# Hybrid attention block: q and k of a pair of heads as seven block products, computed ahead of attention

## The chip, the cores and the metric

One Trainium2 chip, one core of it. The metric is the device time of one execution of the program, in microseconds (us); the median of the runs is compared. Engines are named as in the profile: PE is the matrix engine, PEld its weight load, DVE the vector engine, ACT the scalar engine, POOL the GpSimd engine, SP the engine whose queue issues most DMAs.

## The reference

One decoder layer on x of 1024 tokens by 1024 channels, float32. What matters here:

```
h = rms_norm(x, attn_norm_w)
q, k, v, u, g = split(h @ w_in)            # 1024, 1024, 1024, 2048, 2048 columns
q, k = rms_norm over each 64 columns       # 8 heads, each with two 64-wide halves
p = softmax(q1 k1 / 8 + bias) - lam * softmax(q2 k2 / 8 + bias)     # causal
a = rms_norm(p @ v) * 0.2 ;   y_a = a @ w_proj_attn
c = silu(layer_norm(causal_depthwise_conv(u_a * sigmoid(u_b), 31 taps))) ;  y_b = c @ w_proj_conv
x = x + (sigmoid(g_a) * y_a + sigmoid(g_b) * y_b) @ w_out
x = x + (silu(gate) * up) @ w_down         # of rms_norm(x); 2816 wide
```

## The kernel before

**Numbers.** Each float32 operand of a product is kept as a high and a low part in the matrix engine's reduced type: `split_hi` is a copy on ACT (L120), `low` a subtraction on DVE (L125) or, while `low_by_pool` is set, on POOL (L131). A product is then three matmuls, high by high, high by low and low by high (`mm3`, L168 to L170). `hT_hi` and `hT_lo` hold the normalized input, transposed, in on-chip memory.

**Order of the work.** `first_stage` is a generator; the loop around it gives the depthwise convolution `due += 3.25` steps at every yield. It computes v in four items of 256 columns (`v_item`; V0 in `opening`), then u: the first 128 columns plainly, and the rest in seven `u_pair`s. A `u_pair` already uses a block scheme: the input's channels and tokens are split in two halves each, and seven block products of sums (`TS`, made once by `sums_of_h`) and of weight sums take the place of eight. Then come `Q0` (q and k of head 0) and `V3`. After that attention runs 64 steps, one for each head and each block of 128 queries, in the order of `ORDER`.

**q and k.** `q_item(h)` makes the 256 columns of one head by `gemm_N`: 8 token tiles, 8 channel tiles, 3 matmuls each, 128x256. ACT copies the result out of PSUM (L797) and makes 32 sums of squares (L800), DVE scales by the reciprocal root (L807), and `turn_qk` transposes on PE (L815, tile pQ), scales and splits, and moves half partitions by DMA on SP's queue. `late` holds these turns until their tiles are free.

**An attention step.** `scores(h, i)`: two halves, for each of them matmuls into one of three PSUM tiles `sc` (L1289, L1290), bias and running minimum on DVE (L1291), exponential on ACT (L1296); then both halves are combined on DVE (L1306). `turn` transposes the block of the step before (pT, L1328) and splits it; `weigh` multiplies by v after every second block (pW); `back` and `subln` normalize. Between them `more` puts one or two items of `fill`, which is the list `later`: Q1 to Q7 and the sixteen gates G0 to G15 (`g_item`, 128x512 matmuls, two halves of 24), so that PE has work while a step's softmax runs. The scheduler may move instructions against the program's order, by its own timeline, except where `after` holds them.

**Convolution.** Eight channel blocks, each one load, one first tap on ACT (L588) and 30 taps on DVE (L594, 240 in all); `add_tile` adds a finished block by a DMA on POOL's queue. The accumulator of the first `CONV_PSUM = 4` blocks lies in PSUM, in banks that attention's `sc` tiles take over when `bg.until((NKT - CONV_PSUM) * (CW + 1) - 1)` has drained them. The rest of the taps are spread over the attention steps by each step's estimated slack.

**Weights.** `ws` is the queue of weight tiles, loaded on SP's queue and split ahead of use; `wtiles` rotates three pairs `whi`, `wlo`.

Of the kernel before, what the change touches and what calls it, by code (L numbers as in the profile page):

```python
# [10 lines left out]
F32 = mybir.dt.float32  # L11
# [5 lines left out]
P = 128  # L17
# [40 lines left out]
def kernel(  # L58
# [48 lines left out]
    sm.tile([P, 32], F32, name="pad_sm", bufs=1)  # L107
# [148 lines left out]
    def vectors():  # L256
# [5 lines left out]
        dve.tensor_scalar(pcol("kn"), pcol("kn"), -(HD ** -0.5), None, op0=ALU.mult)  # L262
# [21 lines left out]

    def wtiles():
        return [wp.tile([P, 1024], F32R, tag=t_, name=nm(t_)) for t_ in ("whi", "wlo")]
# [89 lines left out]
    def gemm_N(o, halves, shi, slo, i):  # L376
# [8 lines left out]
    v_lo = [dr.tile([S, 256], F32, name=f"v_lo{j}") for j in range(4)]  # L385
    a_d = [dr.tile([P, S], F32, name=f"a_d{h}") for h in range(H)]
# [16 lines left out]
    last = ["Q0", "V3"]  # L403
    later = [
        ["Q1", "G0", "G1"],
        ["Q2", "G2", "G3"],
        ["Q3", "G4"],
        ["Q4", "G5", "G6"],
        ["Q5", "G7"],
        ["Q6", "G8", "G9"],  # L410
        ["Q7", "G10"],
        ["G11", "G12", "G13", "G14"],
        ["G15"],
    ]

    def loads_of(it):
        c = int(it[1:])
        if it[0] == "V":
            return ld_wide(win, [(V0 + 256 * c, 256)])
        if it[0] == "Q":  # L420
            return ld_wide(win, [(Q0 + c * P, P), (K0 + c * P, P)])
# [4 lines left out]
    for it in ["U0"] + first + last + [x_ for l_ in later for x_ in l_]:  # L426
        ws.plan(loads_of(it))
# [138 lines left out]
    CONV_PSUM = 4  # L566
# [67 lines left out]
    def g_item(c):  # L634
        w = ws.next()
        for sb in range(2):
            o = gemm_T(w, hT_hi, hT_lo, sb)
            sg = wp.tile([P, 512], F32, tag="sg", name=nm("sgg"), bufs=2)
            act.activation(sg[:], o[:], AF.Identity, bias=pcol("gate_b", c))
            nc.sync.dma_start(g_d[c][:, sb * 512 : (sb + 1) * 512], sg[:])  # L640
            yield


    def rsq(v, n, fast):

        r = sm.tile([P, 16], F32, tag="r", name=nm("r"))[:, :n]
        t = sm.tile([P, 16], F32, tag="t", name=nm("t"))[:, :n]
# [32 lines left out]
    def rstd_of(ss, n, scale, fast=False):  # L680
        v = sm.tile([P, 16], F32, tag="v", name=nm("v"))[:, :n]
# [104 lines left out]
    def q_item(h):  # L786
        halves = [ws.next(), ws.next()]
        t = {}
        T[h] = t
        for b in (1, 0):  # L790
            raw = qkp.tile([P, 4, 256], F32, tag="qkraw", name=nm("qkraw"), bufs=2)
            ss = sm.tile([P, 16], F32, tag="ss16", name=nm("ss16"))
            for i2 in range(2):
                o = pg()
                for e in range(2):
                    gemm_N(o[:, 256 * e : 256 * (e + 1)], halves, hT_hi, hT_lo, 4 * b + 2 * i2 + e)
                act.copy(raw[:, 2 * i2 : 2 * i2 + 2, :], o[:].rearrange("p (e c) -> p e c", c=256))  # L797
                jk = sm.tile([P, VD], F32, tag="jk", name=nm("jk"), bufs=1)[:, :HD]
                for g in range(8):
                    act.activation(  # L800
                        jk, o[:, g * HD : (g + 1) * HD], AF.Square, accum_out=ss[:, 8 * i2 + g : 8 * i2 + g + 1]
                    )
                if i2 == 0:
                    yield
            r = rstd_of(ss[:], 16, 1.0 / HD, fast=h > 0)
            r4 = raw[:].rearrange("p i (g d) -> p (i g) d", d=HD)
            dve.tensor_tensor(r4, r4, r.unsqueeze(2).to_broadcast([P, 16, HD]), op=ALU.mult)  # L807

            def turn_qk(z, key, b, raw):


                dma = nc.sync.dma_start
                pt = pm("pQ")
                for i in range(4):
                    pe.transpose(pt[:, i * P : (i + 1) * P], raw[:, i, z * P : (z + 1) * P], ident[:])  # L815
                w = pcol(key + "n")

                def part(j):
                    return qkp.tile([P, 512], F32R, tag=f"{key}s{j}", name=f"{key}s{j}_{h}_{b}", bufs=2 if key == "q" else 3)

                s1, s2 = part(1), part(2)
                act.activation(s1[:], pt[:], AF.Identity, scale=w)
                lo = part(3) if key == "q" else qkp.tile([P, 512], F32R, tag="klo", name=f"klo_{h}_{b}", bufs=1)
                dve.scalar_tensor_tensor(lo[:], pt[:], w, f32(s1[:]), op0=ALU.mult, op1=ALU.subtract)
                if key == "q":
                    dma(f32(s2[HD:, :]), f32(s1[HD:, :]))
                    lo2 = part(4)
                    for one, two in ((s1, s2), (lo, lo2)):
                        if one is lo:
                            dma(f32(two[HD:, :]), f32(one[HD:, :]))  # L830
                        dma(f32(two[:HD, :]), f32(one[HD:, :]))
                        dma(f32(one[HD:, :]), f32(one[:HD, :]))
                    t["q", b] = (s1, lo), (s2, lo2)
                else:
                    act.activation(s2[HD:, :], pt[HD:, :], AF.Identity, scale=w[HD:, :])
                    dma(f32(s2[:HD, :]), f32(lo[HD:, :]))
                    dma(f32(s1[HD:, :]), f32(lo[:HD, :]))
                    t["k", b] = s1, s2

            for z, key in ((1, "k"), (0, "q")):
                free = NT * (h - 1) + (0 if key == "k" and b else NT if key == "q" and not b else NT // 2)
                late.append((free if h else 0, lambda a_=(z, key, b, raw): turn_qk(*a_)))
            yield

    inatt = [False]
    MAKE = {"V": v_item, "U": u_item, "Q": q_item, "G": g_item}
# [179 lines left out]

    def first_stage():
# [6 lines left out]

        def weights_ahead():
            yield
            ws.ahead = 1
            ws.fetch()  # L1040
            yield
# [17 lines left out]
        for c in range(1, NKT):  # L1059
            ahead = ups[c] if c < NKT - 1 else weights_ahead()  # L1060
            next(ahead)
            A = yield from u_pair(c, A, ahead)
        st_ctx.close()
        tt_ctx.close()
# [8 lines left out]
        v_tiles[0] = v3_tiles  # L1073
        load_bias(0)
        ws.ahead = 2
        yield from run(last[:1])
        bg.until((NKT - CONV_PSUM) * (CW + 1) - 1)
        yield from run(last[1:])
# [155 lines left out]
    for _ in first_stage():  # L1234
# [7 lines left out]
        due += 3.25  # L1242
# [5 lines left out]
    low_by_pool[0] = False  # L1248
# [10 lines left out]
    V, AN, SSA, PT, ES, RL = {}, {}, {}, {}, {}, {}  # L1259

# [10 lines left out]
    def scores(h, i):  # L1271
# [7 lines left out]
        for j in range(2):  # L1279
            qh, ql = t["q", i // 4][j]  # L1280
            e = aps.tile([P, S], F32, tag="E", name=nm("E"), bufs=4)
# [16 lines left out]
            )  # L1298
        if h not in RL:
# [59 lines left out]
    def subln(h):  # L1359
        an = AN[h]  # L1360
        r = rstd_of(SSA[h][:], NT, 1.0 / VD, fast=True)
        dve.tensor_tensor(an[:], an[:], r.unsqueeze(2).to_broadcast([P, NT, VD]), op=ALU.mult)
# [26 lines left out]
    fill = run(it for l_ in later for it in l_)  # L1389
    plan = [sum(4 if it[0] == "Q" else 2 for it in l_) for l_ in later]  # L1390
# [744 lines left out]
```

## Time and profile before

| | |
|---|---|
| median of 3 runs | 1727.1 us (1726.74 to 1728.84) |
| profiled execution, span from first to last instruction | 1725.7 us; the page gives it no other time |
| PE busy | 1714.6 us, 99% of the span |
| DVE busy | 1275.4 us, 74% |
| ACT busy | 862.5 us, 50% |
| POOL busy | 219.1 us, 13% |

How to read it: the busy share is an average over stages. "Windows" are stretches of the span, with busy time of each engine in each. A group row gives line, engine, operation, output and inputs, count, then busy time and mean ns of one, then the idle time before it and what ended that. A matmul's record is longer than the time after which the next one starts, so for PE the spacing of starts in the timeline is the price of one.

### The profile page before, as it was taken

Reading aid. Unit: us, or ns where it says so; the run is one execution under the profiler, and the core shown is the slowest. Engines: PE = TensorE matmul, PEld = TensorE weight load, DVE = VectorE, ACT = ScalarE, POOL = GpSimd, SP = SyncE. Lnnn points to the kernel's source line nnn. Section 1 sums busy time; section 2 is a strip of 40 time slices with the busy share of each in tenths; the row PEclk is TensorE's granted clock in tenths of the full one; section 3 lists DMA queues with packets and bytes.
Section 4 is the critical chain, followed back from the end, with each engine's and each line's share of the span. In section 5 each row is a group of like instructions: output and inputs, shape, how many; then the busy total and the mean of one; then the engine's idle time right before and its main releaser. Section 6 shows DMA issues by size and latency. Waiting matters only on the chain.

```text
span 1725.7 us, 25863 instructions
## 1 busy us (share of the span) xinstructions
PE 1714.6 (99%) x9243; PEld 1477.9 (86%) x9243; DVE 1275.4 (74%) x2128; ACT 862.5 (50%) x1958; POOL 219.1 (13%) x207
## 2 busy tenths in 40 slices
PE   9999999999999999999999999999999999999999
PEld 7997889998998998988788888888888888888887
DVE  7675889898988888878687769966676666575544
ACT  5333335767777776756556325633333333333332
POOL 3997851000000000000000000000000000000000
PEclk9999999999999999999999999999999999999999
DMA  6344445336345344343973683245455445598663
GB/s 208 116 126 132 131 151 154 104 109 171 104 127 147 115 125 138 101 136 130 333 238 118 200 296 119 74 135 164 147 170 170 154 141 164 175 355 285 217 215 130
DMA packets 261604, 281.64 MB, mean 163 GB/s; under 512 B 16546, under 2 KB 181986, under 8 KB 261475
## 3 DMA queue, kind: packets, MB, share of 16 engines
q1 hardware_dynamic: 254160, 267.71, 48.3%
q0 software_dynamic: 5680, 9.39, 2.6%
q10 hardware_dynamic: 1634, 2.89, 0.5%
q8 instruction: 73, 1.20, 0.3%
q14 instruction: 57, 0.46, 0.1%
HBM read 181.84 MB, written 85.50 MB: 155 GB/s over the span
## 4 chain that ended last, share of the span: by engine, by line
PE 92%; DMA 3%; DVE 2%; ACT 1%; issue 1%; POOL 0%; SPq 0%; DVEq 0%; POOLq 0%; ACTq 0%
PE acc L980 29%; PE acc L488 12%; PE pg L168 12%; PE pg L169 12%; PE pg L170 12%; PE wo L1850 3%; PE sc L1290 2%; PE sc L1289 2%; PE pT L1328 2%; PE pg L1106 1%; DVE acc L594 1%; PE pW L168 1%; PE pW L169 1%; PE pW L170 1%; PE pQ L815 1%
## 5 line engine op out<-in xcount | busy, mean ns | idle before, releaser
L594 DVE SCALAR_TENSOR_TENSOR acc<-u,cw,acc 128x1023 f32<-128x1023 f32 (+14 forms) x240 | 303.4, 1264 | 23.2 <-ACT acc L588 20.7
L170 PE MATMUL pg<-whi,hT_lo 128*128 128x256 f32 x704 | 200.2, 285 | 0.0
L168 PE MATMUL pg<-whi,hT_hi 128*128 128x256 f32 x704 | 199.7, 285 | 0.4 <-DVE v L125 0.4
L169 PE MATMUL pg<-wlo,hT_hi 128*128 128x256 f32 x704 | 199.5, 284 | 0.0
L125 DVE TENSOR_TENSOR wlo<-draw,whi 128x1024 fp32r<-128x1024 f32 x75 | 91.7, 1223 | 83.4 <-ACT whi L120 78.9
L120 ACT CAST whi<-draw 128x1024 fp32r<-128x1024 f32 x75 | 79.1, 1055 | 129.5 <-PE acc L488 114.3
L169 PEld LDWEIGHTS pg<-wlo,hT_hi 128*128 128x128 f32 x704 | 134.4, 191 | 1.8
L170 PEld LDWEIGHTS pg<-whi,hT_lo 128*128 128x128 f32 x704 | 134.3, 191 | 1.8
L168 PEld LDWEIGHTS pg<-whi,hT_hi 128*128 128x128 f32 x704 | 134.0, 191 | 2.1 <-DVE v L125 0.6
L120 ACT CAST whi<-wraw 128x1024 fp32r<-128x1024 f32 x90 | 94.7, 1052 | 70.6 <-PE pg L169 32.6
L488 PE MATMUL acc<-wlo,whi 128*128 128x512 f32 x308 | 119.8, 389 | 0.0
L488 PE MATMUL acc<-whi,wlo 128*128 128x512 f32 x308 | 119.8, 389 | 0.0
L1296 ACT ACTIVATE E<-E,mn 128x640 f32<-128x640 f32 (+7 forms) x128 | 99.8, 781 | 30.8 <-DVE mn L1291 29.2
L168 PE MATMUL pg<-hT_hi,whi 128*128 128x512 f32 x288 | 114.4, 397 | 0.1
L169 PE MATMUL pg<-hT_lo,whi 128*128 128x512 f32 x288 | 113.7, 395 | 0.0
L170 PE MATMUL pg<-hT_hi,wlo 128*128 128x512 f32 x288 | 113.7, 395 | 0.0
L120 ACT CAST whi<-s 128x1024 fp32r<-128x1024 f32 x54 | 56.9, 1053 | 104.9 <-PE acc L980 101.8
L125 DVE TENSOR_TENSOR wlo<-wraw,whi 128x1024 fp32r<-128x1024 f32 x75 | 93.3, 1246 | 12.6 <-ACT whi L120 12.3
L1291 DVE CUSTOM_DVE_ANT_0 E<-sc,tb 128x512 f32<-128x512 f32 (+3 forms) x128 | 74.2, 585 | 33.2 <-PE pT L1328 16.1
L980 PE MATMUL acc<-h_hi,whi 128*128 128x512 f32 x240 | 93.4, 389 | 0.0
L980 PE MATMUL acc<-h_lo,whi 128*128 128x512 f32 x240 | 93.4, 389 | 0.0
L980 PE MATMUL acc<-h_hi,wlo 128*128 128x512 f32 x240 | 90.1, 389 | 0.0
(370 smaller groups left out, 4589.7 us busy)
## 6 DMA issues: line engine op xcount, KB each, us to landing
wraw<-in_w_gate_up_dram SPq DMA_DIRECT2D x44, 512.0 KB, 4.7
wraw<-in_w_in_dram SPq DMA_DIRECT2D x38, 512.0 KB, 4.0
qs<-qs SPq DMA_DIRECT2D x96, 128.0 KB, 2.3
wd<-in_w_down_dram SPq DMA_DIRECT2D x44, 256.0 KB, 3.1
tdT<-wd SPq DMA_DIRECT2D x88, 128.0 KB, 4.8
draw<-sdS SPq DMA_DIRECT2D x44, 256.0 KB, 3.7
draw<-tdT SPq DMA_DIRECT2D x44, 256.0 KB, 3.7
wraw<-in_w_in_dram SPq DMA_DIRECT2D x32, 256.0 KB, 3.3
```

What stands on the lines that cost most here:

```text
L120: act.copy(dst, src)
L125: last_lo[0] = dve.tensor_tensor(dst, src, f32(hi), op=ALU.subtract).ins
L168: pe.matmul(o, lh, rh, start=start, stop=False)
L169: pe.matmul(o, lh, rl, start=False, stop=False)
L170: last_mm[0] = pe.matmul(o, ll, rh, start=False, stop=stop).ins
L488: m = pe.matmul(o[s_][i][:], l_[:, ts], r_[:, 512:], start=start and j + y_ == 0, stop=j == n - 1 and y_ == 2, skip_group_check=not start,)
L594: dve.scalar_tensor_tensor(a_, us[c][:, : S - n], cw[:, c, t : t + 1], a_, op0=ALU.mult, op1=ALU.add)
L980: last_mm[0] = pe.matmul(o[:], a_[x_][:, k, :], b_[y_][:, k, :], start=start and k + x_ + y_ == 0, stop=k == 3 and x_ == 1, skip_group_che ...
L1289: pe.matmul(o[:, :w], qh[:, qs], k, start=True, stop=False)
L1291: dve.tensor_tensor_reduce(e[:, ks], o[:, :w], tb[:, S - nk + c0 : S - nk + c0 + w], 1.0, mn[:, j : j + 1] if c0 else 3.0e38, ALU.add, ALU ...
L1296: act.activation(e[:, :nk], e[:, :nk], AF.Exp, bias=mn[:, j : j + 1], scale=-1.0, accum_out=l[:, j : j + 1])
L1850: last_mm[0] = pe.matmul(o[s_][i][:], A[u_], B[v_], start=start and j + y_ == 0, stop=j == 3 and y_ == 2, skip_group_check=not start,).ins
```

## The change

Seven things, which go together.

1. `Q` items leave the list of fill work. A new stage `q_stage` between the last `u_pair` and `V3` computes q and k of two heads at a time (`q_pair`), by seven block products (`QSEVEN`) with the sums `TS` that the `u_pair`s use. A product is 4 token tiles by 4 channel tiles by 3 matmuls of 128x256. Sums of weights and the low parts are made on POOL (on DVE at the start of the first pair). Its `yield`s come after each product, so the convolution gets its 3.25 steps 28 times more.
2. The results go to memory (`qk_d`, 512 KB for a head and half of the tokens), with sums of squares by one Square on ACT and one reduction on DVE for each half. The reciprocal roots are made on DVE for six heads at once and for two (`qk_roots`).
3. Attention loads them back (`qk_load`, at steps 0 and 3 of the head before), scales them on POOL one step later (`qk_norm`), and turns them with the same `turn_qk`.
4. `later` is the sixteen gates alone. `g_item` yields after a quarter of a half (6 matmuls), and `more` runs once in the middle of `scores` and once behind it.
5. `turn` comes two steps behind `scores`, not one. Two weight tiles (`whi2`, `wlo2`) serve as fifth and sixth `E` tile, and the weights of attention rotate over two pairs.
6. `low_by_pool` stays set through attention, and `subln` multiplies on POOL, but for the last head.
7. `CONV_PSUM` is 6.

```diff
-        dve.tensor_scalar(pcol("kn"), pcol("kn"), -(HD ** -0.5), None, op0=ALU.mult)
+        dve.tensor_scalar(pcol("qn"), pcol("qn"), -0.125, None, op0=ALU.mult)
+        dve.tensor_scalar(pcol("kn"), pcol("kn"), 0.125 * HD ** -0.5, None, op0=ALU.mult)
...
     def wtiles():
-        return [wp.tile([P, 1024], F32R, tag=t_, name=nm(t_)) for t_ in ("whi", "wlo")]
+        z = next(wplace[0])
+        return [wp.tile([P, 1024], F32R, tag=f"{t_}{z}", name=nm(t_), bufs=1) for t_ in ("whi", "wlo")]
...
-    last = ["Q0", "V3"]
-    later = [["Q1", "G0", "G1"], ...
+    last = ["V3"]
+    later = [f"G{c}" for c in range(2 * NKT)]
...
-    CONV_PSUM = 4
+    CONV_PSUM = 6
...
     def g_item(c):
...
+                mm3(o[:], w[0][:, k, :], w[1][:, k, :], hT_hi[:, k, cs], hT_lo[:, k, cs], k == 0, k == NKT - 1)
+                if k % 2 and k < NKT - 1:
+                    yield
...
+    def qk_load(h, b):
+        raw = qkp.tile([P, 4, 256], F32, tag="qkraw", name=f"qkraw{h}_{b}", bufs=2)
+        nc.sync.dma_start(raw[:].rearrange("p i c -> p (i c)"), qk_d[h][b][:])
...
+    def qk_norm(h, b, raw):
+        r = rs[:, 32 * h + 16 * b : 32 * h + 16 * b + 16]
+        r4 = raw[:].rearrange("p i (g d) -> p (i g) d", d=HD)
+        (pool if h else dve).tensor_tensor(r4, r4, r.unsqueeze(2).to_broadcast([P, 16, HD]), op=ALU.mult)
...
+    QSEVEN = (
+        ("11", (0, 0), "b"),
+        ("12", (1, 0), "a"),
+        ("S2", 2, "b"),
+        ("S1", 1, "c"),
+        ("S3", 3, "b"),
+        ("S4", (1, 1), "c"),
+        ("22", 4, "b"),
+    )
...
+        def keep(k):
+            h, b = 2 * c + k[0], k[1]
+            t_ = out[k]
+            nc.sync.dma_start(qk_d[h][b][:], t_[:].rearrange("p i c -> p (i c)"))
+            for e in range(2):
+                jk = wp.tile([P, 512], F32, tag="sg", name=nm("qsq"), bufs=2)
+                act.activation(jk[:], t_[:, 2 * e : 2 * e + 2, :].rearrange("p i c -> p (i c)"), AF.Square)
...
+        for z, (a_, b_, s_) in enumerate(QSEVEN):
...
+            for i in range(4):
+                ts = slice(i * P, (i + 1) * P)
+                e, w = i // 2, slice(256 * (i % 2), 256 * (i % 2 + 1))
+                for k in range(4):
+                    for x_, y_ in ((0, 0), (0, 1), (1, 0)):
+                        last_mm[0] = pe.matmul(
+                            o[s_][e][:, w], Bz[x_][:, k, ts], hi_lo[y_][:, k, :],
...
+            if z == 0:
+                take((0, 0), "b")
+                if c == 0:
+                    less(raw["S1"], raw["21"], raw["22"], ALU.add, dve)
+                    less(raw["21"], raw["11"], raw["21"], eng=dve)
+                less(raw["11"], raw["S1"], raw["11"], eng=pool if c else dve)
+                low_by_pool[0] = c > 0
+                A["S2"] = q_split(raw["11"])
+                low_by_pool[0] = True
+            elif z == 1:
+                plus((0, 0), "a")
+                keep((0, 0))
+                A["S1"] = q_split(raw["S1"])
+            elif z == 2:
+                take((0, 1), "b")
+                A["S3"] = q_split(raw["21"])
+                less(raw["12"], raw["12"], raw["11"])
...
         st_ctx.close()
+        yield from q_stage()
...
     while late:
         late.pop(0)[1]()
-    low_by_pool[0] = False
     pcv_ctx.close()
...
+            if j == 0:
+                scm.append(last_mm[0])
+                amid()
...
-        dve.tensor_tensor(an[:], an[:], r.unsqueeze(2).to_broadcast([P, NT, VD]), op=ALU.mult)
+        eng = pool if h < H - 1 else dve
+        eng.tensor_tensor(an[:], an[:], r.unsqueeze(2).to_broadcast([P, NT, VD]), op=ALU.mult)
...
-        scores(h, i)
+        if h + 1 < H and n % NT in (0, 3):
+            raws[n % NT == 0] = qk_load(h + 1, int(n % NT == 0))
+        if h + 1 < H and n % NT in (1, 4):
+            qk_norm(h + 1, int(n % NT == 1), raws[n % NT == 1])
+        scores(h, i, lambda: more(p))
         scm.append(last_mm[0])
-        more((p + 1) // 2)
-        if n:
-            hp, ip = steps[n - 1]
+        more(p)
+        if n > 1:
+            hp, ip = steps[n - 2]
             turn(hp, ip)
```

More of the change, by code (lines that the diff above doesn't have):

```diff
@@ L784 @@
     late = []
[L786 to L845, printed above, removed]
@@ L1388 @@
     scm, weighs, backs, sublns = [], [], [], []
[L1389 to L1390 removed]
+    fill = run(later)
     def more(k):
[L1394 removed]
+        with after(scm[-7] if len(scm) >= 7 else None):
             for _ in range(k):
@@ L1468 @@
     n = len(steps)
+    wplace[0] = cycle((0, 1, 2))
+    turn(*steps[-2])
     group()
```

237 lines of the change are left out of this document (196 added, 41 removed).

## The prediction, made before the changed kernel was run

> **What bounds the kernel now.** I read the page's first parts, then windows, then single instructions in order of time.
>
> ```profile
> span 1725.7 us, 25863 instructions
> PE 1714.6 (99%) x9243; PEld 1477.9 (86%) x9243; DVE 1275.4 (74%) x2128; ACT 862.5 (50%) x1958; POOL 219.1 (13%) x207
> PE 92%; DMA 3%; DVE 2%; ACT 1%; issue 1%; POOL 0%; SPq 0%; DVEq 0%; POOLq 0%; ACTq 0%
> ```
>
> PE is busy 99% of the span and carries 92% of the chain that ended last. A busy PE may still be a waiting one, so the windows around the change, and PE's own waits in attention, come next (columns: stretch, then PE, PEld, DVE, ACT, POOL busy, the granted clock, DMA share and rate).
>
> ```profile
> 147.00:247.00 100.00, 100.00 (x447) 82.56 (x447) 84.54 (x79) 37.17 (x50) 72.48 (x45) 1.00 0.39 118
> 297.00:822.00 525.00, 522.13 (x3487) 477.30 (x3486) 447.48 (x985) 370.37 (x1215) 21.06 (x74) 1.00 0.45 128
> ...
> PE sc L1289 <- DMA ks<-klo: 1.1, 1, 1.1
> PE sc L1290 <- DMA qs<-qs: 0.8, 1, 0.8
> ```
>
> The stretches are the last five pairs of u, and attention; Q0 and V3 lie between. The granted clock is 1.00 in both. In attention PE's two long waits for others make 1.9 us in 525, while DVE is busy 85% and POOL almost idle. So a matmul removed here is time removed, as long as the other engines keep up.
>
> **The change, part by part. The products.** Price of one matmul: the spacing of starts.
>
> ```profile
> 65.98 0.28 PE L168 MATMUL pg<-whi,hT_hi 128*128 128x256 f32 x1
> 66.10 0.28 PE L169 MATMUL pg<-wlo,hT_hi 128*128 128x256 f32 x1
> 66.22 0.28 PE L170 MATMUL pg<-whi,hT_lo 128*128 128x256 f32 x1
> ...
> L170 PE MATMUL pg<-whi,hT_lo 128*128 128x256 f32 x704 | 200.2, 285 | 0.0
> ```
>
> A 128x256 matmul starts 0.12 us after the one before. The last row, one of three alike, has 3 x 704 = 2112 of them: 8 heads x 8 x 8 x 3 = 1536 for q and k, and 576 for V1 to V3. Afterwards there are 4 pairs x 7 products x 4 x 4 x 3 = 1344, of the same shape with the same roles. The difference of 192 at 0.12 us is **23.0 us** off PE. Transposes, scores, weighing and gates keep their counts. The moved part, 1344 of Q1 to Q7 at 0.12 us = 161 us, leaves attention, which keeps 525 - 161 = 364 us of PE work, 5.7 us a step in place of 8.2.
>
> **The new stage's other engines.** It lasts 28 products of 48 x 0.12 = 5.76 us, 161 us. In a pair of 40.3 us, POOL makes seven low parts and five sums of 128x1024, ACT seven splits, eight copies and eight squares, DVE six additions and eight reductions besides 3.25 convolution steps a product.
>
> ```profile
> L131 POOL TENSOR_TENSOR wlo<-s,whi 128x1024 fp32r<-128x1024 f32 x10 | 24.5, 2450 | 7.1 <-ACT whi L120 7.1
> L594 DVE SCALAR_TENSOR_TENSOR acc<-u,cw,acc 128x1021 f32<-128x1021 f32 (+29 forms) x58 | 73.6, 1269 | 5.1 <-ACT acc L588 3.8
> L1000 DVE TENSOR_TENSOR p<-acc,p 128x512 f32<-128x512 f32 x5 | 3.4, 686 | 0.0
> L120 ACT CAST whi<-wraw 128x1024 fp32r<-128x1024 f32 x6 | 6.3, 1056 | 10.1 <-PE acc L980 10.1
> ...
> 53.84 0.29 DVE L273 TENSOR_REDUCE lsum<-lprod 128x2 f32<-128x128 f32 x1
> ```
>
> POOL: 12 x 2.45 = 29 us of 40.3, the share it had beside the u pairs, where PE stayed at 100%. ACT: 7 x 1.06 + 16 copies or squares at about 0.6 (estimate from the 1.06 for twice the columns) = 17 us. Three rotating pairs of tiles let a split start two products, 11.5 us, before its use; split and low part take 3.5. So this work costs PE nothing; without that lead it would cost up to 3.5 us a product. The writes of the results (512 KB each) have no reader for dozens of microseconds.
>
> DVE until attention may start: taps sit in PSUM banks that the scores take over, so 6 x 30 = 180 taps must be done.
>
> ```profile
> 0.00:247.00 247.00, 114.28 (x90) 1.00 0.45 137
> 297.00:822.00 525.00, 155.37 (x124) 1.00 0.45 128
> ```
>
> These windows count taps alone: 90 by the end of u. So 90 more must go into 161 us of new stage and 23 us of V3 (192 x 0.12), 184 us. By start times a tap takes some 1.19 us (records overlap by 0.07): 107 us. Beside them come 24 additions (0.69, 16 us), 32 reductions of 512 columns (the trace has one of 128, 0.29 us, so between that and four times it; I take the 0.69 of an addition over as many columns: 22 us, with 9 and 37 as ends), and some 19 us of sums for the first pair, roots, scaling and splits: 164 of 184, or 179 at the dear end. It fits, and the cover is V3; each 1.2 us that it runs over is paid by PE.
>
> At the seam from u to the new stage, S2 of the first pair has to wait for loads, three DVE sums, a split and a low part, some 1.2 x 4 + 1.1 = 6 us behind data and queued taps, against two products, 11.5 us. That may miss: between 0 and 6 us, I take **+2**.
>
> **Attention.** What leaves DVE and ACT (groups of this stage):
>
> ```profile
> L125 DVE TENSOR_TENSOR wlo<-wraw,whi 128x1024 fp32r<-128x1024 f32 x30 | 36.6, 1219 | 2.8 <-ACT whi L120 2.7
> L807 DVE TENSOR_TENSOR qkraw<-qkraw,r 128x1024 f32<-128x1024 f32 x14 | 17.0, 1218 | 0.0
> L1362 DVE TENSOR_TENSOR an<-an,r 128x1024 f32<-128x1024 f32 x7 | 8.5, 1216 | 0.0
> L800 ACT ACTIVATE jk<-pg 128x64 f32<-128x64 f32 x210 | 47.5, 226 | 4.5
> L800 ACT ACTIVATION_READ_ACCUMULATOR jk<-pg 128x1 f32 x211 | 42.1, 200 | 0.0
> L797 ACT COPY qkraw<-pg 128x512 f32<-128x512 f32 x26 | 15.3, 589 | 7.8 <-PE pg L170 7.7
> ```
>
> DVE: 447 - 37 - 17 - 8 - 12 (small steps of Q's roots), and taps fall from 124 to about 43 (240 - 180, less those that the spare 20 us take), another 102 off. That leaves 271, with the overlap of records about 280 of 364 us, 77%. ACT loses 47 + 42 of squares, 15 of copies and 14 splits of Q's weights at 1.06: 370 becomes about 250 of 364. Neither is near PE, if nothing else happens.
>
> But POOL gets about 36 operations of 128x1024 here: 15 low parts of gate weights, 14 scalings, 7 of subln. What POOL does to DVE can be seen once:
>
> ```profile
> 271.12 4.77 POOL L131 TENSOR_TENSOR wlo<-wraw,whi 128x1024 fp32r<-128x1024 f32 x2 [17.17 <-ACT whi L120]
> ...
> 271.60 1.95 DVE L657 TENSOR_TENSOR r<-r,t 128x16 f32<-128x16 f32 x1
> 273.47 1.26 DVE L594 SCALAR_TENSOR_TENSOR acc<-u,cw,acc 128x1009 f32<-128x1009 f32 x1
> 274.65 2.31 DVE L807 TENSOR_TENSOR qkraw<-qkraw,r 128x1024 f32<-128x1024 f32 x1
> ...
> 287.70 1.22 DVE L807 TENSOR_TENSOR qkraw<-qkraw,r 128x1024 f32<-128x1024 f32 x1
> ```
>
> While two POOL operations run (271.12 to 275.89), a DVE operation on 16 columns takes 1.95 us, not 0.17, and a scaling 2.31, not 1.22, each ending with or just after a POOL operation; the tap between them, whose accumulator lies in PSUM, is untouched at 1.26. So two POOL operations cost DVE 1.78 + 1.09 = 2.9 us, 1.4 each. In attention the combination of the halves (64) and the taps into on-chip memory are of the kind that waits. 36 x 1.4 = 50 us: DVE goes from 280 to 330 of 364, 91%.
>
> What that costs PE has no row. Lower bound 0: between 200 and 240 us DVE was busier than that and PE never idle,
>
> ```profile
> 200.00:210.00 10.00, 10.00 (x45) 8.28 (x45) 9.70 (x9) 2.16 (x3) 6.40 (x5) 1.00 0.91 247
> ...
> 200.00:240.00 40.00, 40.00 (x178) 33.11 (x178) 37.09 (x35) 13.36 (x19) 27.15 (x17) 1.00 0.42 122
> ```
>
> 93% (37.09 of 40). Upper bound: attention needs DVE at no more than the 85% it had, so 330 / 0.85 = 388 us, 24 over. Attention has shorter waits to hide than u, but tiles turned two steps behind have 11 us for a chain of scores, minimum, exponential and combination. I stay near the row that shows such a load: **+5**.
>
> The Trainium skill ("SBUF — State Buffer", section "Who interferes with whom") says that DVE and GpSimd share a port pair as an exclusive lock, and that a DVE instruction with two SBUF inputs contends with a GpSimd instruction that reads SBUF, the later one blocking fully. By that rule the two waits here, 1.78 and 1.09 us, are parts of a POOL operation, and the trace agrees that the tap into PSUM goes free; if each wait were whole, the sum would be the 1718 of the rival "DVE sets the pace" below, and by the rows it is 1709.
>
> The two DMA waits of turned q and k (1.1 + 0.8) go, since the turns no longer hang on products finished in the same head: **-2**. Next late would be the loads from memory, covered by one step of 5.7 us:
>
> ```profile
> wraw<-in_w_in_dram SPq DMA_DIRECT2D x38, 512.0 KB, 4.0
> L1319 POOL MEMSET pl<- 128x128 f32 x31 | 6.4, 206 | 448.7 <-PE pW L169 357.1 <-PE pW L170 38.1 <-DVE rl L1304 20.5
> L578 POOL DMA_DIRECT2D cs_d<-c_d x5 | 5.1, 1028 | 51.2 <-DMA c_d<-acc 38.7 <-DMA c_d<-done 12.5
> ```
>
> 512 KB lands in 4.0 us; a load sits in SP's queue ahead of the turns' DMAs and delays those by an issue. Uncovered it would be 14 x 4. POOL's memsets wait for weighing (357 us) and its accumulating DMAs for a finished channel block (51), and scalings and low parts are now queued behind those. A gate's low part is made a gate ahead, four steps; a scaling has three steps before its head. I take 0, at most one missed step, 6 us.
>
> **Sum** against the profiled execution: 1725.7 - 23.0 + 2 + 5 - 2 = 1707.7. The median shown stands 1.4 us above that span, so **1709 us**.
>
> **The rivals.**
> *Nothing is lost* (1702): neither the seam nor the sharing costs PE anything, 1727.1 - 23.0 - 2. For it: 93% DVE beside a PE that never idles. Against: attention's short waits.
> *DVE sets the pace* (1718): all 36 POOL operations stand in full, 36 x 2.4 = 87 us, so DVE needs 367 of 364 us; at the 97% of its busiest tenth beside u (9.70 of 10 us from 200 to 210) that is 378, 14 over in place of 5. For it: the two caught rows. Against: most waits are partial.
> *The saving is eaten* (1728): the change does on PE what it says and nothing in time, since DVE needs its 85% (24 over, above, in place of 5).
> *Slower: scores wait for the accumulators* (1756). If the 48 POOL operations of the new stage caught a DVE operation each at 1.4 us, 67 us would come onto 164, 231 against 184: attention starts 47 us late, 1709 + 47. It decides from 20 us of spare plus 18 of gain, 38 us or 27 caught operations. Against: 58 taps beside a POOL busy 72% took 1.27 us, as elsewhere; only the first pair's sums, scalings and roots are of the caught kind.
>
> **How the numbers follow.** Forecast (1703 to 1714) 0.60, nothing lost 0.15, DVE sets the pace 0.12, eaten 0.05, slower 0.08. A change within 0.2%, 3.5 us, cannot be told from none. Faster: 0.60 + 0.15 + 0.12 = 0.87; same 0.05; slower 0.08. The range 1700 to 1722 takes in the first three, 0.87 before their tails, and leaves the last two out.
>
> **What would show it.** Right: about 8% fewer PE records of the q and k shape (1344), at 0.12 us; PE without idle through the new stage; attention at 365 to 375 us; combinations (L1306 before, 814 ns) visibly longer in the mean. Wrong: gaps before the third product of the first pair; a gap between V3 and the first scores that ends with a tap; attention over 380 us with DVE above 95%; or scores waiting for the DMAs of turned tiles.

## The result, and the profile after

The changed kernel takes **1773.2 us** in the median of 4 runs (1772.27 to 1779.24), against 1727.0 us (1726.74 to 1728.84) for the kernel before on the same chip: a ratio of 1.0275, 95% interval 1.0258 to 1.0292. It is slower; the forecast was 1709, within 1700 to 1722.

The page of the changed kernel: span, busy times, the granted clock in 40 slices, and the chain by engine.

```profile
span 1770.5 us, 25144 instructions
PE 1716.6 (97%) x9051; PEld 1465.6 (83%) x9051; DVE 1293.8 (73%) x2085; ACT 819.5 (46%) x1461; POOL 400.7 (23%) x281
...
PEclk9999999999998999999999999999999999999999
...
PE 81%; DVE 8%; DMA 5%; ACT 3%; issue 2%; SPq 1%; POOL 0%; DVEq 0%; ACTq 0%; POOLq 0%
```

PE has 192 matmuls fewer (9051 for 9243) and yet is busy 2 us longer; it carries 81% of the chain, not 92%, and DVE, DMA and ACT have entered it. A busy PE is a waiting or slow one here.

Where the stages begin and end, by the first records of a kind (start, duration, then what the engine waited for). The first scores of the changed kernel, and the first matmul of the projection behind attention, in the timeline:

```profile
450.53 0.47 PE L1469 MATMUL sc<-ks,qs 128*128 128x512 f32 x1 [0.46 <-DMA ks<-klo]
...
864.23 0.50 PE L167 MATMUL pg<-aTh,whi 128*128 128x512 f32 x1 [0.87 <-ACT whi L119]
```

The same of the kernel before, the first from the tile view of its scores (the first of two times is the first start), the second from the timeline:

```profile
L1289 PE MATMUL sc<-ks,qs x192: 220/389/499, 306.8 to 798.8; 128*128 128x512 f32 x96, 128*128 128x128 f32 x32, 128*128 128x256 f32 x32, 128*128 128x384 f32 x32
```

```profile
822.56 0.40 PE L168 MATMUL pg<-aTh,whi 128*128 128x512 f32 x1
```

Attention starts 143.7 us later (450.5 for 306.8), lasts 413.7 us in place of 515.8, so 102.1 less, and what follows it takes 906.3 in place of 903.1 us, 3.2 more. 143.7 - 102.1 + 3.2 is the 44.8 us between the two spans.

Against that the plan of the change: moving 1344 matmuls of 0.12 us ahead of attention should start it 161.3 us later, less the 23.0 of Q0, so 138.3, and shorten it by 161.3. The start came 5.4 us later than that, and attention stayed **59.2 us longer** than planned. Part of both is a shift of work: by the count of matmuls, 85 of Q1's ran ahead of the first scores in the kernel before, and 36 of the gates' do in the changed one, so attention had 159.3 us of PE work less, not 161.3.

How much of it is lost time on PE: I counted the matmuls that start in a stage, each at the usual spacing of starts of its shape (0.227 us for 512 columns, 0.173 for 384, 0.12 for 256, 0.109 for 128), and subtracted that from the stage's length. What is left, "lost" from here on, is 6.8 us in attention before and **64.0 us** after. The work counted is 509.0 us before and 349.8 after, 8.0 and **5.5 us of PE work a step**. Counted in the same way, the stretch between u and the first scores lost 0.6 us before and 8.4 after. So the -23.0 became +44.8 by 7.8 us more lost ahead of attention, 57.2 more in it and 3.2 behind it, within half a microsecond. The windows of the same stages show it too (columns as in the prediction): the new stage, V3, attention.

```profile
247.00:416.00 169.00, 164.02 (x1335) 163.12 (x1335) 151.64 (x158) 70.91 (x97) 102.05 (x44) 0.98 0.43 131
416.00:440.00 24.00, 24.00 (x204) 24.00 (x203) 19.94 (x34) 9.30 (x13) 5.80 (x5) 1.00 0.99 316
...
451.00:865.00 414.00, 375.27 (x2118) 317.53 (x2118) 331.45 (x794) 269.82 (x695) 100.03 (x104) 0.98 0.51 149
```

In attention PE is without a record for 38.7 of 414 us; before it was 2.9 of 525. No other engine is near its limit: DVE 80%, where it had 85% before, ACT 65%, POOL 24%. PE's own waits, by what ended them (us in total, times, longest):

```profile
PE sc L1469 <- DMA ks<-klo: 12.3, 7, 4.5
PE sc L1469 <- DVE mn L1471: 5.3, 9, 1.1
PE pW L167 <- DVE pl L124: 4.3, 5, 1.5
PE pQ L821 <- DVE pl L124: 3.7, 2, 2.2
PE pW L167 <- DVE rl L1486: 3.7, 2, 1.9
PE qo L1110 <- ACT whi L119: 3.1, 1, 3.1
PE qo L1110 <- POOL wlo L130: 1.9, 1, 1.9
```

The last two are the seam; the others lie in attention, and no single one has more than 12.3 us. They are all links of one step: turned k through DMA, the running minimum, the split of the transposed block, the normalization. The chain of the changed kernel shows one head's start:

```profile
545.81 0.58 ACT ks L828
546.39 0.70 ACT E L1476 x2
547.09 0.35 ACT jk L1540 x2
547.44 0.32 ACT E L1476
547.76 7.28 DMA ks<-klo
...
555.08 0.79 PE sc L1469
```

The turned k of the next head leaves ACT at 546.4 and the transfers end at 555.0; PE has nothing else to do by 552 and waits. The last transfer took 7.28 us, where the 28 of its kind in attention take 2.3 in the median: other transfers ran beside it, and between 543 and 550 us the DMA share stands above 1 (windows in the last section), against 0.51 over the stage. How much of the lost time is this crowding, no run separates.

### The profile page after: what moved, and what is told of

The parts are those of the page before. It is cut to its first block, busy times and chain, and to the rows that moved or that the text cites. A ratio compares the mean times of both kernels' runs of the same rounds, so it can differ in the third digit from the quotient of the medians.

```text
span 1770.5 us, 25144 instructions
## 1 busy us (share of the span) xinstructions
PE 1716.6 (97%) x9051; PEld 1465.6 (83%) x9051; DVE 1293.8 (73%) x2085; ACT 819.5 (46%) x1461; POOL 400.7 (23%) x281
## 4 chain that ended last, share of the span: by engine, by line
PE 81%; DVE 8%; DMA 5%; ACT 3%; issue 2%; SPq 1%; POOL 0%; DVEq 0%; ACTq 0%; POOLq 0%
PE acc L979 29%; PE acc L480 12%; PE qo L1110 7%; PE pg L167 7%; PE pg L169 7%; PE pg L168 7%; PE wo L2041 3%; DVE acc L587 3%; PE sc L1469 1%; DMA ks<-klo 1%; PE sc L1470 1%; PE pg L1280 1%; PE pT L1511 1%; DVE E L1471 1%; DMA early<-a_d 1%
## 5 line engine op out<-in xcount | busy, mean ns | idle before, releaser
L587 DVE SCALAR_TENSOR_TENSOR acc<-u,cw,acc 128x1023 f32<-128x1023 f32 (+14 forms) x240 | 309.9, 1291 | 22.7 <-ACT acc L581 18.9
L119 ACT CAST whi<-draw 128x1024 fp32r<-128x1024 f32 x75 | 79.1, 1055 | 129.5 <-PE acc L480 120.9
L130 POOL TENSOR_TENSOR wlo<-wraw,whi 128x1024 fp32r<-128x1024 f32 x43 | 107.2, 2494 | 97.8 <-ACT whi L119 96.3
L1469 PE MATMUL sc<-ks,qs 128*128 128x512 f32 (+2 forms) x192 | 73.1, 384 | 17.9 <-DMA ks<-klo 12.3
L1476 ACT ACTIVATE E<-E,mn 128x1024 f32<-128x1024 f32 (+7 forms) x86 | 66.9, 779 | 39.1 <-DVE mn L1471 34.0
L480 PE MATMUL acc<-whi 128*128 128x512 f32 x308 | 84.1, 389 | 0.0
L124 DVE TENSOR_TENSOR wlo<-s,whi 128x1024 fp32r<-128x1024 f32 x40 | 49.0, 1225 | 28.2 <-ACT whi L119 28.2
L480 PEld LDWEIGHTS acc<-whi 128*128 128x128 f32 x308 | 57.8, 188 | 12.0
L480 PEld LDWEIGHTS acc<-whi,wlo 128*128 128x128 f32 x308 | 57.8, 188 | 12.0
L480 PEld LDWEIGHTS acc<-wlo,whi 128*128 128x128 f32 x308 | 57.8, 188 | 12.0
L1470 PE MATMUL sc<-ks,qs 128*128 128x512 f32 (+2 forms) x192 | 66.4, 353 | 0.0
```

The source lines that it names most:

```text
L119: act.copy(dst, src)
L124: last_lo[0] = dve.tensor_tensor(dst, src, f32(hi), op=ALU.subtract).ins
L130: pool.tensor_tensor(dst, src, f32(hi), op=ALU.subtract)
L480: m = pe.matmul(o[s_][i][:], l_[:, ts], r_[:, 512:], start=start and j + y_ == 0, stop=j == n - 1 and y_ == 2, skip_group_check=not start,)
L587: dve.scalar_tensor_tensor(a_, us[c][:, : S - n], cw[:, c, t : t + 1], a_, op0=ALU.mult, op1=ALU.add)
L1469: pe.matmul(o[:, :w], qh[:, qs], k, start=True, stop=False)
```

## The experiments

Two theories from the traces. *Cover* (C in the expectations): q and k were what PE did while a step's chain ran; with 5.5 us of work a step the chain shows. *Sharing* (A): POOL's 36 operations slow DVE and with it the chain. Beside them the expectations name B, that DVE has too much work for the shorter stage, D, that the scheduler's fixed order no longer fits, and single late links: the turned tiles, the loads, the taps, the order of the gates in a step. Where an expectation gives work per step as 5.7, 5.9, 7.0, 8.4 or 8.2, that is the prediction's rougher count over the wider window.

All times are medians; the kernel before ran at 1726.4 to 1727.0 beside them. "Attention" and "lost" are worked out as above from the one execution that was profiled, which stands up to 4.3 us from the median (e3 and e8 4 below, e2 and e4 3 above); they are in us.

| kernel | time | ratio to before (95%) | attention | lost | PE work a step |
|---|---|---|---|---|---|
| before | 1727.0 | | 515.8 | 6.8 | 8.0 |
| after | 1773.2 | 1.0275 (1.0258, 1.0292) | 413.7 | 64.0 | 5.5 |
| e1_all_dve | 1787.7 | 1.0348 (1.0322, 1.0375) | 427.5 | 77.7 | 5.5 |
| e2_norm_dve | 1793.4 | 1.0389 (1.0373, 1.0404) | 439.7 | 90.0 | 5.5 |
| e3_few_taps | 1769.3 | 1.0245 (1.0229, 1.0260) | 405.4 | 55.7 | 5.5 |
| e4_turn_one | 1805.3 | 1.0456 (1.0441, 1.0472) | 448.3 | 98.6 | 5.5 |
| e5_double_fill | 1885.1 | 1.0922 (1.0904, 1.0940) | 529.0 | 5.7 | 8.2 |
| e6_no_pool | 1757.5 | 1.0181 (1.0166, 1.0197) | 400.7 | 51.0 | 5.5 |
| e7_early_turns | 1791.1 | 1.0376 (1.0356, 1.0397) | 428.8 | 79.1 | 5.5 |
| e8_seam | 1775.3 | 1.0283 (1.0264, 1.0303) | 410.7 | 61.0 | 5.5 |
| e9_fill_and_half | 1815.5 | 1.0519 (1.0500, 1.0537) | 454.3 | 19.0 | 6.8 |
| e10_before_thin | 1695.5 | 0.9816 (0.9799, 0.9833) | 480.6 | 124.1 | 5.6 |
| e11_no_pool_few_taps | 1750.8 | 1.0135 (1.0119, 1.0151) | 388.9 | 39.2 | 5.5 |
| e12_fill_behind_turn | 1772.3 | 1.0264 (1.0247, 1.0280) | 414.3 | 64.6 | 5.5 |

**POOL's work given back to DVE.** e1_all_dve gives back the scalings, the multiplication of `subln` and the gates' low parts; e2_norm_dve the scalings alone.

```diff
-        (pool if h else dve).tensor_tensor(r4, r4, ...
+        dve.tensor_tensor(r4, r4, ...                      # e1 and e2
-        eng = pool if h < H - 1 else dve
+        eng = dve                                          # e1
+    low_by_pool[0] = False
     pcv_ctx.close()                                        # e1
```

> The changed kernel, but in attention the scalings of q and k, subln's scaling and the low parts of the gates' weights run on DVE again, as before. Theory A (POOL): these POOL operations hold DVE up and, queued behind POOL's other waits, bring the turned q and k late; without them PE's stalls in attention fall by half or more: 1773 - 35, 1725 to 1745 us. Theory B (DVE has too much work beside a shorter PE): DVE gets 36 x 1.2 = 43 us more, so slower, 1785 to 1815 us. Theory C (too little PE work per step to cover the chain of a step): within 10 us of 1773.

> The changed kernel, only the scaling of q and k on DVE. Theory A, late turns: PE's waits for the DMAs of turned k (12 us in attention) go, with the half-clock stretches behind them: 1745 to 1758 us. Theory B: 14 x 1.2 = 17 us more on DVE, 1778 to 1792. Theory C: 1768 to 1778.

Both are slower than the changed kernel, by 14 and 20 us. With this work off POOL the loss in e1 grew from 64 to 78 us, so the sharing isn't the main cause: DVE's own 1.2 us for each of these operations costs more than the sharing does. Cover alone would have left both near 1773; e1 came out in the range of theory B, and e2 just above it, so work added to DVE does cost time here. Why e2, which moves less, loses more than e1 was not settled.

**The suspected costs taken away.** e3_few_taps leaves 2 of 30 taps in the last two channel blocks. e6_no_pool has no POOL arithmetic in attention: scalings and `subln`'s multiplication are left out, and a low part is a second ACT copy. e11 is both.

```diff
-        return [first_tap] + [tap(t) for t in range(CW - 2, -1, -1)]
+        return [first_tap] + [tap(t) for t in (range(CW - 2, -1, -1) if c < CONV_PSUM else (CW // 2, 0))]   # e3, e11
+        if low_by_pool[0] and inatt[0]:              # e6, e11
+            act.copy(dst, src)
...
-        (pool if h else dve).tensor_tensor(r4, r4, ...
+        if not h:                                    # e6, e11
+            dve.tensor_tensor(r4, r4, ...
...
-        eng.tensor_tensor(an[:], an[:], ...
+        if h == H - 1:                               # e6, e11
+            dve.tensor_tensor(an[:], an[:], ...
```

> The changed kernel with only 2 of 30 DVE taps for the convolution's last two channel blocks (the convolution's output is then another): some 54 taps, 70 us of DVE, leave attention. Theory B: attention comes down to its PE work, 1725 to 1740 us. Theory A: DVE has more room after each block by POOL, but turned q and k stay late: 1750 to 1765. Theory C: 1765 to 1773.

> The changed kernel without POOL's arithmetic in attention: the scalings of q and k (but for head 0) and of subln (but for head 7) are left out, and the low part of a gate's weights is a second copy on ACT, so the output is another; nothing is added to DVE. Theory A: DVE's combinations come back from 0.97 to 0.81 us and turned q and k earlier, 1730 to 1750 us. Theory C: shorter waits only at the margin, 1760 to 1773.

> The changed kernel without POOL's arithmetic in attention and with 2 of 30 taps for the last two channel blocks (both as in the runs that did one of them): DVE and POOL are far from full. If gaps come from how busy DVE and POOL are: 1715 to 1735 us. If they come from the length of a step's chain, at whatever load (theory C): 1745 to 1757 us.

Fewer taps bring 4 us (its interval overlaps that of the changed kernel), no POOL work 16, both 22. So e3 stays far above the 1725 to 1740 of theory B, e6 lies between the ranges of sharing and of cover, and e11 in that of cover. The attention of e6 and of e11:

```profile
452.00:853.00 401.00, 372.93 (x2116) 319.28 (x2115) 302.75 (x790) 281.35 (x713) 16.33 (x70) 0.97 0.51 152
```

```profile
452.00:841.00 389.00, 369.03 (x2117) 317.12 (x2117) 253.77 (x743) 281.22 (x706) 15.45 (x69) 0.98 0.54 157
```

In e11 DVE is busy 65% and POOL 4%, and PE still has no record for 20 of 389 us and loses 39.2. With most of what was suspected gone, more than half of the added loss (39.2 - 6.8 = 32.4 of 57.2) stands.

**The cover given back.** e5_double_fill does every gate matmul twice (768 more of 0.227 us, 174 us of PE work), e9_fill_and_half every second group (87 us). POOL's work, the loads, the turns and the lag stay as in the changed kernel; only PE has more to do between them.

```diff
-                mm3(o[:], ..., k == 0, k == NKT - 1)
+                for twice in range(2):                       # e5
+                    mm3(o[:], ..., k + twice == 0, k + twice == NKT)
+                for twice in range(1 + k % 2):               # e9
+                    mm3(o[:], ..., k == 0, k + twice == NKT)
```

> The changed kernel with every matmul of the gates issued twice into the same sum (the gates are then others): 768 more 128x512 matmuls at 0.227 us, 174 us of PE work that does nothing but fill attention's steps, 8.4 us a step in place of 5.7. Theory C (too little PE work per step): the 55 us by which attention's PE gaps grew go, 1773 + 174 - 55, so 1880 to 1905 us. Theory A (POOL holds DVE up, late turns) and theory D (the scheduler's fixed order no longer fits what the chip does): the gaps stay, 1930 to 1950 us.

> The changed kernel with every second matmul group of the gates issued twice (the gates are then others): half of the filler of the run with all of them doubled, 87 us, 7.0 us of PE work a step. Theory C with a gradual loss: the 58 us of gaps fall to between a third and a half, 1773 + 87 - 35, so 1815 to 1835 us. If there is a sharp threshold near the 8.2 us of before: hardly less than now, 1845 to 1860. If the threshold lies below 7.0: 1800 to 1812.

Both times lie in the ranges that cover gave. The attention of e5 and of e9:

```profile
451.00:991.00 540.00, 538.89 (x2934) 461.38 (x2933) 349.15 (x807) 286.11 (x710) 99.15 (x105) 1.00 0.40 119
```

```profile
451.00:906.00 455.00, 445.10 (x2497) 380.25 (x2496) 328.49 (x800) 275.86 (x701) 99.07 (x104) 1.00 0.46 135
```

PE is without a record for 1.1 of 540 us in e5, 9.9 of 455 in e9, 38.7 of 414 in the changed kernel. The 174 us of matmuls that e5 added to the stage lengthened it by 115; 86 in e9 by 41. The lost time falls from 64.0 over 19.0 to 5.7 as the work of a step goes from 5.5 over 6.8 to 8.2 us, and the kernel before lies on that curve with 6.8 at 8.0. PE's waits in e5's attention (from 452 to 980 us) are these two:

```profile
PE pW L167 <- ACT ph L119: 0.7, 1, 0.7
PE pW L168 <- DVE pl L124: 0.3, 1, 0.3
```

The waits for turned k, the minimum and the normalization are gone and that for the split is down to 0.3 us, though each of those transfers and operations is still there. A longer stage also gives DVE more time, but that does not explain it: DVE is busy 65% of the stage in e5 as in e11, and e11 loses 39.2 us. That is the cover theory, shown; the gaps that theories A and D would have kept are gone.

**The same removal in the kernel before.** e10_before_thin takes the kernel before and multiplies only the first of eight channel tiles in the gates (32 halves, each 21 matmuls of 0.227 us fewer, 152 us), so PE has 5.6 us a step with none of the change's seven parts.

```diff
-            o = gemm_T(w, hT_hi, hT_lo, sb)
+            o = pg()
+            cs = slice(sb * 512, (sb + 1) * 512)
+            mm3(o[:], w[0][:, 0, :], w[1][:, 0, :], hT_hi[:, 0, cs], hT_lo[:, 0, cs], True, True)
```

> The kernel before, with only the first of the eight channel tiles in each gate's product (the gates are then others): 32 x 21 matmuls of 128x512, 152 us of PE work, leave attention and no other engine gains or loses anything; 5.9 us of PE work a step. Theory C: attention's cover goes in this kernel too, without POOL's part, without two steps' lag, without loads from memory, so it gets back far less than 152 us: 1630 to 1670 us. If the changed attention itself (POOL, lag, loads) makes the gaps: 1575 to 1590 us.

Its attention in the windows:

```profile
306.00:787.00 481.00, 409.68 (x2744) 369.52 (x2743) 435.27 (x976) 358.60 (x1199) 19.62 (x73) 0.92 0.47 132
```

and PE's longest waits there, for the whole span:

```profile
PE sc L1291 <- DVE mn L1293: 13.9, 14, 2.2
PE pg L168 <- ACT sgg L641: 8.4, 7, 2.4
PE pT L1330 <- DVE E L1308: 5.9, 7, 1.5
```

152 us of matmuls less gave 31 us back (1727.0 to 1695.5), less than either theory had said. PE now waits for the running minimum, for ACT to read a gate out of PSUM, and for the combination. So a loss needs no POOL work, no loads and no later turn: it comes with the missing matmuls. But this run doesn't isolate the chain as e5 and e9 do. DVE does the work that it did, at 90% of the stage: its 435 us are a floor under these 481, so at most 80 of the 152 us could come back. That the loss is larger here than in the changed kernel (124.1 for 64.0 at nearly the same work) fits the heavier DVE and the lag of one step; no run separates them.

**The lag and single links.** e4_turn_one turns one step behind scores; e7_early_turns loads and scales the second half of the next head's q and k a step earlier; e12_fill_behind_turn puts the step's second gate quarter behind `turn` and ahead of `weigh`.

```diff
-        if n > 1:
-            hp, ip = steps[n - 2]
+        if n > 0:                                    # e4
+            hp, ip = steps[n - 1]                    # e4
...
-        if h + 1 < H and n % NT in (0, 3):
+        if h + 1 < H and n % NT in (0, 2):           # e7, qk_load
-        if h + 1 < H and n % NT in (1, 4):
+        if h + 1 < H and n % NT in (1, 3):           # e7, qk_norm
...
         scm.append(last_mm[0])
-        more(p)
...
+        more(p)                                      # e12, behind turn
```

> The changed kernel with the turn one step behind the scores, as before the change. Theory C: the chain of a step must now fit into one step of 5.7 us, so clearly slower, 1790 to 1830 us. Theories A and B: two steps behind hides little of what they see, within 10 us of 1773.

> The changed kernel with the second half's q and k of the next head loaded at step 2 and scaled at step 3 of a head in place of 3 and 4, so that its k is turned a step, 5 us, earlier. If the waits at the heads' starts for the DMAs of turned k (12 us, and half-clock stretches behind them) are a cause by themselves: 1753 to 1763 us. If they are only where a slack-less PE happens to wait: 1768 to 1780.

> The changed kernel with a step's second quarter of a gate between turning and weighing in place of ahead of both, so that weighing does not stand right behind the transposes whose split it reads. PE's waits ahead of weighing and of turned q and k (20 us) should halve: 1758 to 1766 us. If the scheduler's order undoes the difference, or another wait takes its place: 1770 to 1780 us.

Without the second step of lag the kernel takes 32 us more, as cover had it: that part of the change does what it should. Earlier turns cost 18 us, outside both ranges, though the longest wait in total had been that for turned k; PE's waits in e7 show it as long as it was (12.1 us), and waits for splits and for `subln` beside it:

```profile
PE sc L1469 <- DMA ks<-klo: 12.1, 5, 4.1
PE sc L1469 <- DVE mn L1471: 6.6, 10, 1.8
PE pT L1511 <- DVE pl L124: 6.4, 3, 3.1
...
PE pS L1553 <- POOL an L1546: 3.9, 2, 2.7
```

e12 makes no difference. So the place where PE waits is where it happens to stand when it has run out of work; which link ends a step without cover last wasn't settled.

**The seam.** e8_seam loads the two late weight tiles of the first pair on SP's queue and gives out no convolution steps in the first two products.

```diff
-                q_load(raw[key], 1, j, nc.scalar)
+                q_load(raw[key], 1, j)
...
+            RATE[0] = 0.0 if c == 0 and z < 2 else 3.5
```

> The changed kernel with the first pair's second loads on SP's queue in place of ACT's, and no convolution steps given out in the first two products of the new stage (3.5 in place of 3.25 after that). The gap of PE at the seam, 8 us with a half-clock stretch behind it, should go: 1762 to 1767 us; if the gap comes from the chain of sums and not from what stands ahead of it: 1771 to 1776.

No gain (1775.3, interval over that of the changed kernel), and between 260 and 280 us PE is no less idle. That window in e8, and then in the changed kernel:

```profile
260.00:280.00 20.00, 13.70 (x96) 13.21 (x97) 19.82 (x16) 5.98 (x8) 8.99 (x3) 0.83 0.26 82
```

```profile
260.00:280.00 20.00, 15.47 (x107) 15.27 (x108) 19.79 (x17) 7.00 (x10) 9.43 (x4) 0.83 0.25 79
```

DVE is full in that stretch, and behind its sums come a split and POOL's low part. The run doesn't decide between its two causes, because the trace shows that its edit moved neither the way it was meant to: the loads are issued from 252.1 us on, where the changed kernel issues them from 247.8, and six taps still stand on DVE in the 9 to 10 us ahead of the first sum (260.3 us in the changed kernel, 261.6 in e8). What would mend the seam stays open.

No run points to a version that beats the kernel before. With half of q and k (four heads, 768 matmuls of 0.12 us) left in attention as plain products, a step would have (349.8 + 92.2) / 64 = 6.9 us; an estimate from e9's row (19.0 us at 6.8) puts the loss near 18 us, 11 above the kernel before, which eats the 11.5 us that half of the block products save, and the seam comes on top. It was not run.

## Why the prediction was wrong

The step that failed is "What that costs PE": **+5** in attention, between 0 and 24. It measured **+57.2** of lost time (64.0 - 6.8). Behind it stood the sentence "So a matmul removed here is time removed, as long as the other engines keep up". The two long waits of 1.9 us in 525 were read as if nothing else there could matter; they said only that everything else was covered at 8.0 us of matmuls a step. And "keep up" was measured by DVE's share: the row that set the price (93% DVE beside a PE that never idles) comes from the u stage, where no matmul had to wait for DVE; in attention the matmuls of a step wait for what DVE and ACT make in that step or the two before. Even the upper bound took a share of DVE as the limit. The chain itself was held to be hidden by the 11 us of two steps, but its length was never worked out. By the experiments the attention of the changed kernel is bound in the main by the chain of its step, with no engine beside PE busier than 80%; POOL's work and the taps, which lengthen the chain, are worth 22 us together (e11).

Point by point:

- **Products, -23.0: right.** The tile rows of the new stage, three of fifteen:

```profile
L1110 PE MATMUL qo<-whi,hT_hi x192: 277/283/283, 242.4 to 410.8; 128*128 128x256 f32 x192
...
L1110 PE MATMUL qo<-whi,T1h x64: 282/283/415, 262.6 to 399.3; 128*128 128x256 f32 x64
...
L1110 PE MATMUL qo<-whi,T2h x64: 283/283/283, 271.5 to 393.5; 128*128 128x256 f32 x64
```

  The seven products have 3 x 192 of the roles with hT and 12 x 64 with the sums of it, 1344, and the stage's PE work is where it was put.
- **The new stage costs PE nothing: right but for the seam.** The seam was put at +2, between 0 and 6; lost time between u and the first scores went from 0.6 to 8.4 us, **+7.8**. The product that waits isn't the one of the term: in the first pair PE takes S1 (T1 in the rows above, from 262.6 us) ahead of S2 (T2, from 271.5), and waits 3.1 us for S1's split and 1.9 for its low part, which runs on POOL for 2.34 us where the term had 1.2 on DVE. Not in the term either was that PE then runs at half clock, 2.4 us of the 8.4.
- **DVE done with its taps in time: right.** From 416 to 440 us PE is busy 24.00 of 24, and the first scores start with a wait of 0.46 us, for DMA. The accumulators held nothing up, so the rival "Slower: scores wait for the accumulators" gave the sign by a mechanism that didn't occur.
- **DVE's load in attention: right in size by luck, wrong as the limit.** 330 us were put there, 331.45 measured, but two errors cancel in it. The sharing is real and 28 us, not 50, and the rest is 303 us (302.75 in e6's window), not 280: 58 taps stood in the stage, where about 43 were forecast. The groups of the changed kernel in attention, taps, combinations and the step on one column:

```profile
L587 DVE SCALAR_TENSOR_TENSOR acc<-u,cw,acc 128x1021 f32<-128x1021 f32 (+29 forms) x58 | 79.0, 1362 | 0.1
...
L1489 DVE SCALAR_TENSOR_TENSOR E<-E,rl,E 128x640 f32<-128x640 f32 (+7 forms) x43 | 42.9, 997 | 0.6
L1487 DVE SCALAR_TENSOR_TENSOR rl<-rl,neglam,l 128x1 f32<-128x1 f32 x64 | 26.2, 409 | 0.9
...
L1489 DVE SCALAR_TENSOR_TENSOR Ew<-Ew,rl,Ew 128x896 f32<-128x896 f32 (+7 forms) x21 | 19.3, 917 | 0.2
```

  and of the kernel before:

```profile
L1306 DVE SCALAR_TENSOR_TENSOR E<-E,rl,E 128x640 f32<-128x640 f32 (+3 forms) x64 | 52.1, 814 | 0.6
...
L1304 DVE SCALAR_TENSOR_TENSOR rl<-rl,neglam,l 128x1 f32<-128x1 f32 x64 | 13.7, 214 | 0.5
```

  and of e6, which has no POOL arithmetic in attention:

```profile
L1492 DVE SCALAR_TENSOR_TENSOR E<-E,rl,E 128x640 f32<-128x640 f32 (+7 forms) x43 | 35.1, 816 | 0.6
L1492 DVE SCALAR_TENSOR_TENSOR Ew<-Ew,rl,Ew 128x896 f32<-128x896 f32 (+7 forms) x21 | 17.2, 819 | 0.2
L1490 DVE SCALAR_TENSOR_TENSOR rl<-rl,neglam,l 128x1 f32<-128x1 f32 x64 | 14.0, 218 | 0.9
```

  The 64 combinations (42.9 + 19.3) take 10.1 us more than before, the steps on one column 12.5, 58 taps about 6 (1362 ns, against 1264 in e6): 28 us of DVE, and e6 has all three back. What that is worth in time is 16 us in e6, and next to nothing under cover: in e5 the combinations (986 and 921 ns) and the steps on one column (385) are as long as here, and PE loses 5.7 us in all.
- **DMA waits of turned q and k, -2: wrong in sign.** They went from 1.9 us to 12.3 for k alone. The transfers have less time now, since attention's steps are shorter, and one of them was seen to take three times its usual time; the two shares weren't separated.
- **"What would show it".** Of the signs given for wrong, three showed: gaps before the third product of the first pair, attention over 380 us, scores waiting for turned tiles. The condition set beside the second, DVE above 95%, did not: none of the rivals had a stage that is slow with every engine below its limit.

## What to carry to other kernels

A stage in which PE never waits may owe that to the work that one wants to remove: before taking matmuls out of it or moving them ahead, work out how long one turn of the loop's dependent chain is, and what PE has left to do meanwhile. A low share of the other engines is no proof of slack there, and a short list of waits says only that the present work covers the chain. A cheap trial comes first: thin the matmuls in the old kernel, and see how much of the time comes back (here 31 us of 152). Beside it belongs the floor that the other engines set: DVE's own load would have let no more than 80 of them back.

## What the runs showed of the hardware

The granted clock was 1.00 in all windows shown of the kernel before; in the changed kernel it fell to 0.50 in seven stretches ahead of its last 2 us, each 3.41 or 6.83 us long, that begin and end on one grid of 3.41 us. Five windows on that grid, around the head's start shown above:

```profile
543.32:546.73 3.41, 1.49 (x14) 1.28 (x13) 2.99 (x10) 3.41 (x10) 0.00 (x0) 1.00 1.15 240
546.73:550.15 3.42, 3.42 (x19) 3.42 (x18) 2.10 (x5) 2.09 (x7) 0.00 (x0) 0.50 1.12 354
550.15:553.56 3.41, 1.71 (x11) 1.07 (x10) 1.82 (x3) 2.14 (x9) 0.36 (x2) 1.00 0.87 294
553.56:556.97 3.41, 1.89 (x6) 1.60 (x7) 0.63 (x2) 0.00 (x0) 0.00 (x0) 0.50 0.04 9
556.97:560.39 3.42, 3.42 (x11) 2.74 (x10) 1.04 (x6) 0.92 (x2) 0.00 (x0) 0.50 0.00 0
```

Here both full-clock windows in which PE has a record for about half of the time (1.49 and 1.71 of 3.41 us) are followed by one at half clock. In the changed kernel's attention six windows on the grid with full clock were at or below 1.71 us, and five of them were followed by half clock; of those above, none was. Half clock went on for a second window where PE was idle in the first too (1.89 of 3.41), and ended after windows with 2.76 us or more. What ends it is not settled, though: in e10 half clock went on after a window that PE's records fill.

```profile
576.90:580.32 3.42, 3.42 (x14) 2.78 (x12) 3.42 (x12) 3.29 (x14) 0.00 (x0) 0.50 0.54 158
580.32:583.73 3.41, 3.41 (x18) 3.41 (x17) 3.41 (x4) 3.38 (x8) 0.16 (x1) 0.50 0.47 127
```

So gaps of some 2 us in a window can put PE at half speed for 3.4 us or more: 8.4 of the 64.0 us lost fall into such stretches, 34.7 of 98.6 in e4. The Trainium skill ("TensorE: Matmul & The Clock Gate", section "Part 1: The HAM clock gate") says that the clock is halved after an idle window of about 3.4 us, that the window is free-running, and that as much sustained work frees it. The length and the grid agree, and so does the release in the changed kernel, but not at the place of e10; and here a window that is only half idle was enough.
